# A hybrid delta-rule and HGRN2 block: values token-major in the front, pairs within a chunk on strips, keys transposed once for a pair of heads

## The chip, the cores and the metric

The kernel runs on one core of a Trainium2 chip. Five engines work side by side, each with its own queue of instructions: TensorE (PE in the profile, with its weight loads as PEld), VectorE (DVE), ScalarE (ACT), GpSimd (POOL) and SyncE (SP, which only issues DMAs here). They wait for one another through semaphores. The metric is the device time of one execution in microseconds (us).

## The reference

One layer of a hybrid backbone for 512 latent tokens and 256 context tokens, 1024 wide, in fp32:

```python
h_lat = rms_norm(x, norm_mix_g) * (1 + sc1) + sh1          # and h_ctx
(qkv, a_f, a_b, be_f, be_b, g_a, q_b, i_b, f_f, f_b, g_b, m_a, m_b) = split_last(h @ w_in, IN_SIZES)
...
# gated delta rule, chunked, 4 heads of 128, two directions
u_c = u_c - w_c @ s
s_next = gam_end_c * s + k_end_c.T @ u_c
o = qg_c @ s + att_c @ u_c
# HGRN2, chunked, 4 heads of 128, two directions; v = i_b, k = 1 - f
s_next = f_end_c * s + k_end_c.T @ v_c
pair = exp(where(incl, lg_c[i] - lg_c[j], -inf))
att = einsum('ik,jk,ijk->ij', q_c, k_c, pair)
o = (q_c * exp(lg_c)) @ s + att @ v_c
...
y = sigmoid(m_a) * (norm(oa) * silu(g_a)) @ w_up_a + sigmoid(m_b) * (norm(ob) * silu(g_b)) @ w_up_b
x = x + g1 * (y @ w_out)
x = x + g2 * swiglu(rms_norm(x, norm_ffn_g) * (1 + sc2) + sh2)
out = rms_norm(x, final_norm_g)
```

Each direction scans the context first and the latent tokens from the state that this leaves.

## The kernel before

**Projections.** Activations lie feature-major (features on partitions) as a high and a low part, `hhi, hlo` for the 512 latent tokens and `chi, clo` for the context. Every weight block is loaded by SP into one of two `raw` buffers (`split`, L84), rounded by ACT to `hi` (L100), and DVE makes the rest `lo` (L102). `mm3` (L105) then runs three matmuls for each 128 rows of the weight: hi x hi, hi x lo, lo x hi.

**The front**, up to the first key projection. `hhi` and `hlo` are made in eight steps, and in each step six gate projections (numbers 16 to 21) take their share into six banks `pg0`; their weights come as eight tiles `wr`. The 24 gates (two sets of 4 head gates, two of 8 merge gates) go to DRAM (`gdram`) and are read again by the up-projections. Behind it, at a priority put back by 1500 (so that they fill holes), two more gates are made, and sums for the modulation.

**The loops.** Streams are written as generators: `G0` and `G2` (`gdn_pair`, two heads of the delta rule each), `H0` to `H3` (`hgrn`, one head each), `F` (`filler`: one gate by `gate_low`, its matmuls at a priority put back by 1000), `N` and `aT` (modulation weights). The string `PLAN` says how many steps of each are written next; a scheduler then places each engine's instructions by that order, by priorities and by the buffers that come free. At `X` the delta rule's buffers are closed, all gates and modulation sums that are left are queued at low priority, and the rest of H2 runs, alone. Behind it come the up-projections (`pup`), `w_out` and the SwiGLU part (`pf`, `pfo`).

**One HGRN head** (`hgrn`, L484): two forget gates and the query are projected, log gates `L` and keys `K` are made on ACT and DVE. Then a ladder of levels: level 7 is the diagonal, and level l (block b = 1, 2, 4 ... 64) covers those pairs of a chunk of 128 tokens that lie in one block of 2b but not in one of b. For each level `kq` holds scaled keys and queries, `att` (L528) multiplies all 128 x 128 pairs of each of 4 chunks into the bank `pA`, and a predicated copy with the mask `lev` takes those of this level into `AT`; ACT copies the diagonal. After the ladder, `values` (L493) projects the head's values feature-major (24 matmuls of 512 and 24 of 256 columns), copies them, transposes six tiles into `pv` and copies those to `vh`. The scan over chunks then uses `AT` and `vh`.

**One delta-rule pair** (`gdn_pair`): after the inverses come six steps of two heads and two directions (L822 on). Each takes `pk` (a bank): the product of key and state, `rt`, the product with the inverse, then `u` (L837), a transpose of the key tile (L842), its copy scaled by decay (`kend`, L843) and their product (L844), which updates the state. Key tiles are transposed once for each direction. Outputs from `aT` and `u` (L853) go to `oa2`; `head_norm` (L469) squares, scales and transposes them into `pt` and stores y in `ydram`.

Of the kernel before, what the change touches and what calls it, by code (L numbers as in the profile page):

```python
# [13 lines left out]
P = 128  # L14
D = 1024
KT = 8
# [9 lines left out]
LEVELS = (1, 2, 4, 8, 16, 32, 64)  # L26
PADN = 8 * 68 + 260
# [4 lines left out]
        "F:1 G0:99 H0:99 F:3 G2:4 H1:99 G2:4 F:1 G2:99 N:1 H3:99 aT:1 H2:1 X H2:99")  # L32


def shape_constants():
    i = np.arange(P)
    r, c = i[:, None], i[None, :]
    sq = np.concatenate(
        [(r == c), (r <= c), (r >= c), (r < c), (r > c)], axis=1).astype(np.float32)
    lev = [(r // (2 * b) == c // (2 * b)) & (r // b != c // b) for b in LEVELS]  # L40
    return sq, np.concatenate(lev, axis=1).astype(np.uint8)
# [7 lines left out]
def body(tc, T, out, tap=None):  # L49
# [8 lines left out]
    with ExitStack() as root:  # L58
# [71 lines left out]
        ydram = dr.tile([8, P, SEQ], F32, name="ydram")  # L130
        gcols = [C_GA + P * i for i in range(4)] + [C_GB + P * i for i in range(4)]
# [45 lines left out]
        rest = [22, 23] + list(range(16))  # L177
# [3 lines left out]
        with ExitStack() as st:  # L181
# [174 lines left out]
            for d in range(KT):  # L356
# [20 lines left out]
            lev = cp.tile([P, 7 * P], U8, name="lev")  # L377
# [21 lines left out]
            for i in rest[0:2]:  # L399
                w = [s1.tile([P, KT, P], F32R, name=f"rw{i}{j}") for j in range(2)]  # L400
                w = split([W_IN[:, gcols[i]:gcols[i] + P]], KT, P, dst=[t[:, :, :] for t in w])
                gate_out(i, feat(w, lat, SEQ, f"pgate{i}"), sp, "gt")
            for q in quarters[0:4]:
# [80 lines left out]
        def hgrn(h):  # L484
# [8 lines left out]
            def values():  # L493
                w = split([W_IN[:, C_IB + P * h:C_IB + P * h + P]], KT, P)
                Z = hg.tile([P, TOK], F32, name=f"{n}Zv", tag="Z", bufs=2)
                for src, a, t in ((lat, CTX, SEQ), (ctx, 0, CTX)):
                    ps = feat(w, src, t, f"{n}zv_{a}")
                    nc.scalar.copy(Z[:, a:a + t], ps[:, 0:t])
                for g, cnt in ((0, 4), (4, 2)):
                    pv = pmm(f"{n}pv{g}")  # L500
                    for i in range(cnt):
                        nc.tensor.transpose(pv[:, P * i:P * i + P], Z[:, P * (g + i):P * (g + i + 1)], ident)
                    nc.scalar.copy(vh[:, g:g + cnt, :], pv[:, 0:P * cnt].rearrange("p (g k) -> p g k", k=P))

# [21 lines left out]
            AT = hg.tile([P, 4, P], F32, name=n + "AT", tag="AT")  # L526

            def att(kq, lvl):  # L528
                pA = bank("ha", f"{n}pA{lvl}")
                for c in range(4):  # L530
                    nc.tensor.matmul(pA[:, P * c:P * c + P], kq[:, 0, P * c:P * c + P], kq[:, 1, P * c:P * c + P],  # L531
                                     start=True, stop=True)
                if lvl == 7:
                    nc.scalar.copy(AT[:, :, :], pA.rearrange("p (c i) -> p c i", i=P))
                else:
                    nc.vector.copy_predicated(AT[:, :, :], lev[:, P * lvl:P * lvl + P].unsqueeze(1).to_broadcast([P, 4, P]),
                                              pA.rearrange("p (c i) -> p c i", i=P))
# [23 lines left out]
            values()  # L561
# [127 lines left out]
        def gdn_pair(h0):  # L689
# [127 lines left out]
            oa2 = gd.tile([P, 2, 4, P], F32, name=n + "oa", tag="blk", bufs=3)  # L817
            seen = set()
# [368 lines left out]
```

## Time and profile before

| what | before |
|---|---|
| median of 3 runs (lowest to highest) | 1082.74 us (1082.46 to 1085.16) |
| the profiled execution | 1084.9 us, span 1083.2 |
| granted clock, mean | 0.983 |
| first key projection (`g_k_zl`) begins | 102.4 us |
| last transposes of pair 2's norm | 508.5 us |
| first pairs of H2 (`h_pA`) | 545.9 us |
| last transposes of H2's norm | 580.25 us |
| up-projections at full speed | 615.5 us |

The page's windows give, for each stretch, the busy time of each engine and its instructions in brackets, the granted TensorE clock, the share of the DMA engines and what they moved. Rows of the timeline give the start, the length, the engine, the line, the tiles out<-in and the shape; a PE row's length includes the pipeline, so the distance of two starts is the price of one in a row of them. An fp32 product shows two records, a transpose one. The slices of the page (each 27 us, busy share in tenths) show how PE stands over the span:

```profile
PE   4999999889999999899989899999999999999996
```

### The profile page before, as it was taken

What the parts mean: (1) busy time and instruction counts of PE and PEld (TensorE: products, weight loads), DVE (VectorE), ACT (ScalarE), POOL (GpSimd) and SP (SyncE); (2) the same over time, 40 slices, a digit from 0 to 9 for tenths busy, and PEclk for the clock granted to TensorE, in tenths of its full rate; (3) what the DMA queues carried; (4) which work ended last, traced back from release to release, by engine and by line L of the source; (5) the groups of instructions that cost most, each with busy time, mean ns of one, the idle gap of its engine ahead of it and who ended that gap; (6) DMA issues with size and microseconds to landing.
All of it is one profiled execution on the core that took longest, in us unless ns stands there. A gap on an engine that the chain in (4) does not pass through costs nothing.

```text
span 1083.2 us, 16716 instructions
## 1 busy us (share of the span) xinstructions
PE 1018.9 (94%) x6567; PEld 843.8 (78%) x6567; DVE 659.3 (61%) x1246; ACT 549.2 (51%) x1037; POOL 72.4 (7%) x129
## 2 busy tenths in 40 slices
PE   4999999889999999899989899999999999999996
PEld 2587888777897887798767688798888878888785
DVE  3375686789767968875795565777343433422524
ACT  4373678658867765876764643442222222221212
POOL 1000000400001021001101000011000000000000
PEclk9999999989999999999899999999999999999998
DMA  9953222112004123102636643546333323322222
GB/s 315 344 182 114 60 57 61 50 58 69 3 25 142 50 68 88 51 2 96 203 120 220 226 157 119 154 138 192 96 98 94 97 84 98 97 97 97 89 97 87
DMA packets 139649, 121.72 MB, mean 112 GB/s; under 512 B 5533, under 2 KB 116531, under 8 KB 139571
## 3 DMA queue, kind: packets, MB, share of 16 engines
q1 hardware_dynamic: 133923, 104.05, 31.0%
q0 software_dynamic: 3552, 13.11, 3.6%
q10 hardware_dynamic: 2096, 3.50, 1.0%
q8 instruction: 51, 0.84, 0.3%
q14 instruction: 27, 0.22, 0.1%
HBM read 110.16 MB, written 10.49 MB: 111 GB/s over the span
## 4 chain that ended last, share of the span: by engine, by line
PE 43%; DVE 4%; DMA 4%; issue 3%; ACT 3%; POOL 1%; SPq 0%; POOLq 0%; ACTq 0%; DVEq 0%
PE pf L110 22%; PE pfo L110 10%; PE pup L110 3%; DMA uy<-ydram 1%; PE pgate L110 1%; PE pwo L110 1%; PE h_pA L531 1%; DMA mwb<-in_mod_w_dram 1%; DVE lo L102 1%; ACT hi L100 1%; PE p_s_pk L835 1%; PE p_s_pk L844 1%; DVE acc L878 0%; DMA ug<-gdram 0%; PE h_z L110 0%
## 5 line engine op out<-in xcount | busy, mean ns | idle before, releaser
L100 ACT CAST hi<-raw 128x1024 fp32r<-128x1024 f32 (+1 forms) x129 | 127.6, 991 | 274.2 <-PE pf L110 96.6
L102 DVE TENSOR_TENSOR lo<-raw,hi 128x1024 fp32r<-128x1024 f32 (+1 forms) x129 | 148.0, 1147 | 171.0 <-ACT hi L100 170.6
L110 PE MATMUL pf<-hhi,hi 128*128 128x512 f32 (+1 forms) x352 | 133.8, 381 | 0.0
L110 PE MATMUL pf<-hhi,lo 128*128 128x512 f32 (+1 forms) x352 | 133.7, 380 | 0.0
L110 PE MATMUL pf<-hlo,hi 128*128 128x512 f32 (+1 forms) x352 | 133.7, 380 | 0.0
L110 PEld LDWEIGHTS pf<-hlo,hi 128*128 128x128 f32 x352 | 66.2, 188 | 12.7 <-DVE hlo L1067 0.2
L110 PEld LDWEIGHTS pf<-hhi,lo 128*128 128x128 f32 x352 | 66.2, 188 | 12.7 <-DVE lo L102 0.2
L110 PEld LDWEIGHTS pf<-hhi,hi 128*128 128x128 f32 x352 | 66.1, 188 | 12.3
L110 PE MATMUL pfo<-lo,uh 128*128 128x512 f32 x176 | 68.8, 391 | 0.1
L110 PE MATMUL pfo<-hi,ul 128*128 128x512 f32 x176 | 68.5, 389 | 0.0
L110 PE MATMUL pfo<-hi,uh 128*128 128x512 f32 x176 | 67.9, 390 | 0.0
L110 PE MATMUL pgate<-hhi,hi 128*128 128x512 f32 x128 | 52.9, 413 | 4.1 <-ACT hi L100 4.0
L110 PE MATMUL pgate<-hhi,lo 128*128 128x512 f32 x128 | 52.4, 410 | 4.3 <-DVE lo L102 4.3
L110 PE MATMUL pgate<-hlo,hi 128*128 128x512 f32 x128 | 51.9, 405 | 0.0
L1123 DVE TENSOR_TENSOR sg<-sg,pf 128x512 f32<-128x512 f32 x22 | 15.1, 687 | 49.4 <-PE pf L110 49.4
L878 DVE SCALAR_TENSOR_TENSOR acc<-mwb,sc,acc 128x256 f32<-128x256 f32 x72 | 34.4, 480 | 9.9 <-DMA mwb<-in_mod_w_dram 8.6
L110 PE MATMUL h_z<-hhi,hi 128*128 128x512 f32 x96 | 39.7, 413 | 0.0
L110 PEld LDWEIGHTS pfo<-lo,uh 128*128 128x128 f32 x176 | 33.0, 188 | 7.8 <-DVE lo L102 1.0
L110 PE MATMUL h_z<-hlo,hi 128*128 128x512 f32 x96 | 39.0, 406 | 0.0
L110 PE MATMUL h_z<-hhi,lo 128*128 128x512 f32 x96 | 38.5, 401 | 0.0
L110 PEld LDWEIGHTS pfo<-hi,uh 128*128 128x128 f32 x176 | 32.8, 188 | 7.3 <-ACT hi L100 0.7
L110 PEld LDWEIGHTS pfo<-hi,ul 128*128 128x128 f32 x176 | 33.0, 188 | 6.8
(449 smaller groups left out, 2518.4 us busy)
## 6 DMA issues: line engine op xcount, KB each, us to landing
raw<-in_ffn_w_in_dram SPq DMA_DIRECT2D x44, 512.0 KB, 3.8
raw<-in_w_in_dram SPq DMA_DIRECT2D x37, 512.0 KB, 3.7
raw<-in_ffn_w_out_dram SPq DMA_DIRECT2D x22, 512.0 KB, 3.5
mwb<-in_mod_w_dram POOLq DMA_DIRECT2D x18, 512.0 KB, 4.7
mw<-in_mod_w_dram SPq DMA_DIRECT2D x16, 512.0 KB, 6.0
gdram<-gt SPq DMA_DIRECT2D x24, 256.0 KB, 2.2
raw<-in_w_in_dram SPq DMA_DIRECT2D x18, 256.0 KB, 2.9
mwe<-in_mod_w_dram SPq DMA_DIRECT2D x4, 1024.0 KB, 7.7
```

The lines of the kernel that those rows point to most:

```text
L100: nc.scalar.copy(hi[:, :, :], raw[:, :, :])
L102: nc.vector.tensor_tensor(lo[:, :, :], raw[:, :, :], hi.bitcast(F32), op=ALU.subtract)
L110: nc.tensor.matmul(ps, a[u](k), b[v](k), start=(start and n == 0), stop=(stop and n == tot - 1))
L531: nc.tensor.matmul(pA[:, P * c:P * c + P], kq[:, 0, P * c:P * c + P], kq[:, 1, P * c:P * c + P], start=True, stop=True)
L835: nc.tensor.matmul(pk[:, P:2 * P], N[:, d, e, g, :], rt[:, :], start=True, stop=True)
L844: nc.tensor.matmul(pk[:, 2 * P:3 * P], kend[:, :], u[:, :], start=True, stop=True)
L878: nc.vector.scalar_tensor_tensor(acc[:, :], mw[:, k - k0, :], sc[:, k:k + 1], acc[:, :], op0=ALU.mult, op1=ALU.add)
L1123: nc.vector.tensor_tensor(sg[:, :], sg[:, :], pgu[1][:, :], op=ALU.mult)
```

## The change

Three things, and the plan's numbers.

1. *Values.* In the front four of the six `pg0` banks now hold values of all heads: the activations stand still (128 tokens) and 512 columns of the weights for values stream, so the bank is token-major at once. The four gates that stood there (18 to 21) go to the head of `rest`; two of them are made at low priority where gates 22 and 23 were made, and the fillers get four more gates than before (20 for 16). Behind those two gates, at the same priority, the values of the context are made from four weight blocks, 48 matmuls of 128x512 into two banks `pv`. ACT copies the six tiles, SP stores them in `vdram`, and each head loads its own with one DMA into `vh`. The projection, copies and transposes of `values` go.
2. *Pairs.* For levels 0 to 4 and the diagonal `att` now multiplies only the blocks of 32 x 32 on the diagonal of each chunk: 16 products, each with 128 rows of contraction and 32 columns, in four column strips of PE. Level 5 takes the blocks beside them in the same shape, level 6 two blocks of 64 x 64 a chunk (8 products). The predicated copies work on `AD` (128 x 4 x 32); at level 4 four DVE copies put `AD` into `AT`, and levels 5 and 6 are copied by ACT.
3. *Keys of the delta rule.* The six key tiles of each head of a pair are transposed once, ahead of the steps, and copied by ACT (`kt`); the decay goes onto u instead: `ue` is u scaled by a product `nbe` of both factors, and plain `u` is made only where outputs need it.

`PLAN` gets three more fillers before X (12 for 9), and eight gates for seven are left behind it.

```diff
-        "F:1 G0:99 H0:99 F:3 G2:4 H1:99 G2:4 F:1 G2:99 N:1 H3:99 aT:1 H2:1 X H2:99")
+        "F:2 G0:99 H0:99 F:3 G2:4 H1:99 F:1 G2:4 F:2 G2:99 N:1 H3:99 aT:1 H2:1 X H2:99")
...
-        rest = [22, 23] + list(range(16))
+        rest = [18, 19, 20, 21, 22, 23] + list(range(16))
...
-                    nc.sync.dma_start(wr[:, :], W_IN[P * e:P * e + P, C_MB:C_MB + NG0 * P])
+                    nc.sync.dma_start(wr[:, 0:4 * P], W_IN[P * e:P * e + P, C_IB:C_IB + 4 * P])
+                    nc.sync.dma_start(wr[:, 4 * P:], W_IN[P * e:P * e + P, C_MB:C_MB + 2 * P])
...
-                    for i in range(NG0):
-                        nc.tensor.matmul(pg0[i][:, :], u[:, P * i:P * i + P], v[:, d, :],
-                                         start=(d == 0 and n == 0), stop=(d == KT - 1 and n == 2))
-            for i in range(NG0):
-                gate_out(16 + i, pg0[i], sp, "gt")
+                    for i in range(4):
+                        nc.tensor.matmul(pg0[i][:, :], v[:, d, P * i:P * i + P], u[:, 0:4 * P], **ends)
+                    for i in range(4, NG0):
+                        nc.tensor.matmul(pg0[i][:, :], u[:, P * i:P * i + P], v[:, d, :], **ends)
+            def value_out(g, ps):
+                vt = sp.tile([P, NH * P], F32, name=f"vt{g}", tag="gt", bufs=3)
+                nc.scalar.copy(vt[:, :], ps[:, :])
+                nc.sync.dma_start(vdram[g, :, :], vt[:, :])
...
+            pv = [pmm(f"pv{g}") for g in range(2)]
+            for kk in range(4):
+                w = split([W_IN[2 * P * kk:2 * P * kk + 2 * P, C_IB:C_IB + 4 * P]], 2, 4 * P)
+                for g in range(2):
+                    mm3(pv[g][:, :], [lambda k, t=t: t[:, 2 * kk + k, P * g:P * g + P] for t in ctx],
+                        [lambda k, t=t: t[:, k, :] for t in w], 2, start=(kk == 0), stop=(kk == 3))
+            for g in range(2):
+                value_out(g, pv[g])
...
             def att(kq, lvl):
+                w = 64 if lvl == 6 else NB
                 pA = bank("ha", f"{n}pA{lvl}")
                 for c in range(4):
-                    nc.tensor.matmul(pA[:, P * c:P * c + P], kq[:, 0, P * c:P * c + P], kq[:, 1, P * c:P * c + P],
-                                     start=True, stop=True)
+                    for j in range(P // w):
+                        kt0, qt0 = P * c + w * j, P * c + w * (j ^ (lvl in (5, 6)))
+                        nc.tensor.matmul(pA[w * j:w * j + w, w * c:w * c + w], kq[:, 0, kt0:kt0 + w], kq[:, 1, qt0:qt0 + w],
+                                         start=True, stop=True, tile_position=(0, w * j))
...
+                elif lvl < NSM:
+                    nc.vector.copy_predicated(AD[:, :, :], lev[:, NB * lvl:NB * lvl + NB].unsqueeze(1).to_broadcast([P, 4, NB]), pAv)
                 else:
+                    for j in range(P // w):
+                        s = slice(w * j, w * j + w)
+                        nc.scalar.copy(AT[s, :, w * (j ^ 1):w * (j ^ 1) + w], pAv[s, :, :])
+                if lvl == NSM - 1:
+                    for j in range(P // NB):
+                        s = slice(NB * j, NB * j + NB)
+                        nc.vector.tensor_copy(AT[s, :, s], AD[s, :, :])
...
-            values()
+            nc.sync.dma_start(vh[:, :, :], vdram[:, :, P * h:P * h + P].rearrange("g p v -> p g v"))
...
+                for g0, cnt in ((0, 2), (2, 4)):
+                    pt = bank("ga", f"{n}kt{e}{g0}")
+                    for i in range(cnt):
+                        nc.tensor.transpose(pt[:, P * i:P * i + P], KTt[:, g0 + i, :], ident)
+                    nc.scalar.copy(kt[:, g0:g0 + cnt, :], pt[:, 0:P * cnt].rearrange("p (g k) -> p g k", k=P))
...
-                        nc.scalar.activation(u[:, :], pk[:, P:2 * P], AF.Copy, scale=nbkv[:, g, d:d + 1])
+                        if step < 5:
+                            kt, nbe = kts[e]
+                            ue = gd.tile([P, P], F32, name=m + "ue", tag="ke", bufs=3)
+                            nc.scalar.activation(ue[:, :], pk[:, P:2 * P], AF.Copy, scale=nbe[:, g, d:d + 1])
                         if g >= 2:
+                            nc.scalar.activation(u[:, :], pk[:, P:2 * P], AF.Copy, scale=nbkv[:, g, d:d + 1])
...
-                            nc.tensor.transpose(pk[:, 2 * P:3 * P], KTt[:, g, :], ident)
-                            nc.scalar.activation(kend[:, :], pk[:, 2 * P:3 * P], AF.Copy, scale=dec[:, d, 1, g, h:h + 1])
-                            nc.tensor.matmul(pk[:, 2 * P:3 * P], kend[:, :], u[:, :], start=True, stop=True)
+                            nc.tensor.matmul(pk[:, 2 * P:3 * P], kt[:, g, :], ue[:, :], start=True, stop=True)
```

How the change moves instructions is shown at three places; names end in a running number, and lines of the kernel after are higher by some rows. PE, end of the front: before, the last deferred gate (`pgate_741`) goes directly over to `pab`, the projection of decay and beta, which stands ahead of the first key projection.

```order
L110 MATMUL pgate_741<-hhi,rw_735 128x512
L110 MATMUL pgate_741<-hlo,rw_735 128x512
L110 MATMUL pgate_741<-hhi,rw_736 128x512
L418 MATMUL pab_859<-chi,wab_855 32x256
L418 MATMUL pab_859<-clo,wab_855 32x256
```

After, at the same place (`hi_782` and `lo_784` are the first of the four weight blocks):

```order
L113 MATMUL pgate_750<-hhi,rw_745 128x512
L113 MATMUL pv_778<-hi_782,chi 128x512
L113 MATMUL pv_778<-lo_784,chi 128x512
L113 MATMUL pv_778<-hi_782,clo 128x512
L113 MATMUL pv_778<-hi_782,chi 128x512
L113 MATMUL pv_778<-lo_784,chi 128x512
```

46 of the 48 context-value matmuls stand between the gate and `pab`.

PE, the ladder of H2 with gates between its levels; before:

```order
L110 MATMUL pgate_5527<-hhi,lo_5525 128x512
L531 MATMUL h_pA_5943<-h_kqd 128x128 x4
L531 MATMUL h_pA_5954<-h_kq_5949 128x128 x4
L110 MATMUL pgate_5527<-hhi,hi_5523 128x512
L110 MATMUL pgate_5527<-hlo,hi_5523 128x512
L531 MATMUL h_pA_5967<-h_kq_5962 128x128 x4
```

After, the same place:

```order
L113 MATMUL pgate_5819<-hhi,hi_5815 128x512
L550 MATMUL h_pA_6270<-h_kqd 32x32 x16
L550 MATMUL h_pA_6293<-h_kq_6288 32x32 x16
L113 MATMUL pgate_5819<-hlo,hi_5815 128x512
L113 MATMUL pgate_5819<-hhi,lo_5817 128x512
L113 MATMUL pgate_5819<-hhi,hi_5815 128x512
L550 MATMUL h_pA_6318<-h_kq_6313 32x32 x16
```

Each call of `att` has 16 products of 32x32 in place of 4 of 128x128, and the gates between them stay.

ACT, from pair 2's last y (`p_oa<-p_1_pt`) on; before, the copies and exponentials of two projections of H2 stand there, with `h_kqd` still far behind:

```order
L481 ACTIVATE p_oa<-p_1_pt,vc 128x512
L516 ACTIVATE h_sg_5447<-h_sg_5447 128x768
L512 COPY h_Z_5835<-h_z_0_5837 128x512
L541 ACTIVATE h_Ed<-h_K,lno 128x512
L512 COPY h_Z_5835<-h_z_512_5863 128x256
L100 CAST hi_6042<-raw_6040 128x1024
L520 ACTIVATE h_sg_5447<-h_sg_5447 128x768
L522 ACTIVATE h_L<-h_sg_5447,lbo 128x768
```

After, the second forget gate is already copied (`h_Z_6161`), and the first keys (`h_kqd`) come four rows behind y:

```order
L506 ACTIVATE p_oa<-p_1_pt,vc 128x512
L527 ACTIVATE h_sg_6162<-h_Z_6161 128x768
L528 ACTIVATE h_sg_6162<-h_sg_6162 128x768
L529 ACTIVATE h_sg_6162<-h_sg_6162 128x768
L569 ACTIVATE h_kqd<-h_K,lno 128x512
L582 ACTIVATE h_kq_6288<-h_K,lno 128x2x256
L533 ACTIVATE h_sg_6162<-h_sg_6162 128x768
L525 COPY h_Z_6228<-h_z_0_6230 128x512
```

Counted to the last row that the first pairs need (the copy of `h_q` into `h_kqd`, further down), it was 29 rows from y before and is 17 now.

More of the change, by code (lines that the diff above doesn't have):

```diff
@@ L26 @@
 LEVELS = (1, 2, 4, 8, 16, 32, 64)
+NB = 32
+NSM = 5
 PADN = 8 * 68 + 260
@@ L364, in body @@
                 for n, (u, v) in enumerate(((wh, hhi), (wl, hhi), (wh, hlo))):
-                    for i in range(NG0):
-                        nc.tensor.matmul(pg0[i][:, :], u[:, P * i:P * i + P], v[:, d, :],
-                                         start=(d == 0 and n == 0), stop=(d == KT - 1 and n == 2))
-            for i in range(NG0):
-                gate_out(16 + i, pg0[i], sp, "gt")
+                    ends = dict(start=(d == 0 and n == 0), stop=(d == KT - 1 and n == 2))
+                    for i in range(4):
[6 more added lines that the diff above has]
+                nc.sync.dma_start(vdram[g, :, :], vt[:, :])
+            for i in range(4):
+                value_out(2 + i, pg0[i])
+            for i in range(4, NG0):
+                gate_out(12 + i, pg0[i], sp, "gt")
             for d in range(KT):
@@ L491, in hgrn @@
             vh = hg.tile([P, 6, P], F32, name=n + "v", tag="v")
[L493 to L503, printed above, removed]
             for d in range(3):
@@ L925, in run @@
                     break
-        gates = rest[2:]
+        gates = rest
         def filler(n):
```

20 lines of the change are left out of this document (14 added, 6 removed).

## The prediction

> **What bounds the kernel now.** I read the page's head, then the windows (busy time by stage), then the chain of work that ended last.
>
> ```profile
> span 1083.2 us, 16716 instructions
> PE 1018.9 (94%) x6567; PEld 843.8 (78%) x6567; DVE 659.3 (61%) x1246; ACT 549.2 (51%) x1037; POOL 72.4 (7%) x129
> core 0: us, PE busy (x) PEld busy (x) DVE busy (x) ACT busy (x) POOL busy (x), PEclk, DMA share, GB/s
> 0.00:102.40 102.40, 84.95 (x616) 59.21 (x616) 52.13 (x152) 44.46 (x75) 4.84 (x21) 0.98 0.78 247
> 102.40:508.50 406.10, 387.00 (x3221) 332.27 (x3222) 311.90 (x643) 292.12 (x639) 44.96 (x79) 0.98 0.19 55
> 508.50:545.90 37.40, 32.97 (x192) 27.23 (x191) 28.01 (x56) 26.36 (x47) 6.47 (x6) 0.91 0.69 215
> 545.90:565.50 19.60, 16.09 (x96) 13.55 (x97) 19.27 (x35) 13.41 (x19) 1.50 (x2) 0.97 0.36 127
> 581.20:615.50 34.30, 29.59 (x130) 23.84 (x128) 16.57 (x26) 20.98 (x31) 0.00 (x0) 1.00 0.69 233
> 545.23 0.63 ACT h_kqd L544
> 545.90 2.05 PE h_pA L531 x16
> 887.68 65.33 PE pf L110 x288
> ```
>
> The loops from 102.40 (first key projection) to 508.50 (pair 2's last norm) are bound by TensorE: 387.0 us busy of 406.1, so 19.1 idle; DVE and ACT reach 77% and 72%. There an instruction taken from PE is worth its spacing. The tail from 508.50 to 615.50 isn't: head H2 stands alone, its first pairs wait for ACT's keys (545.23), and from 545.90 DVE is busy 19.27 of 19.60. PE's gates fill the holes there. From the up-projections on, nothing is edited. The last row prices a 128x512 matmul: 65.33/288 = 0.227 us.
>
> The sum is made against the profiled execution, 1084.9 us (span 1083.2 and 1.7 around it), which is 0.2% above the median of 1082.74; the difference is carried to the median.
>
> **The change, before 508.50.**
>
> ```profile
> 347.29 0.28 PE L110 MATMUL g_v_zc<-clo,hi 128*128 128x256 f32 x1
> 347.41 0.28 PE L110 MATMUL g_v_zc<-chi,lo 128*128 128x256 f32 x1
> 347.53 1.05 PE L531 MATMUL h_pA<-h_kqd 128*128 128x128 f32 x8
> 348.42 1.06 PE L531 MATMUL h_pA<-h_kq 128*128 128x128 f32 x8
> ```
>
> Starts give 0.12 for a 128x256 matmul, and 0.89 for a call of att: eight records (two passes of four fp32 products) at 0.111. A transpose is one record, and I price it at 0.111 too.
>
> *Values.* In the front four of the six gate banks become values: the same 128x512 shape and count, so nothing changes there. Two of the deferred gates are still made there. New are the context's values: 4 blocks x 2 banks x 2 k x 3 = 48 matmuls, 48 x 0.227 = **+10.9**, and the order puts nearly all ahead of the first key projection, with nothing beside them that they could replace. Removed from each head: 24 x 0.227 + 24 x 0.12 + 6 transposes x 0.111 = 8.99; H0, H1 and H3 lie before 508.50: **−27.0**. Three more fillers (12 for 9) are put there: 3 x 24 x 0.227 = **+16.3**; its ends are 0, if all of them fall into the 19.1 us of PE's idle time, and 16.3. I take the whole, since PE's holes are the short waits between products and a filler behind them is already there. The four gates handed to the fillers balance the four value projections that leave the front, so the net of this part is only the two transposed shapes: 256-wide matmuls and transposes go.
>
> *Keys of the delta rule.*
>
> ```profile
> L842 PE MATMUL p_s_pk<-sq,g_KT 128*128 128x128 f32 x40 | 11.0, 279 | 0.0
> L843 ACT ACTIVATE p_s_ke<-p_s_pk,dec 128x128 f32<-128x128 f32 x40 | 14.6, 372 | 7.4 <-PE p_s_pk L842 7.1
> ```
>
> Forty transposes become 24: 16 x 0.111 = **−1.8**. ACT loses the 40 key copies and 16 of u and gets 40 of ue and 8 for the transposed keys. In 32 places u now stands behind ue on ACT, so its product with aT starts 0.372 later. ACT is 72% busy and the state's own chain takes ue first, so I cost this at nothing; the other streams' matmuls hide it. Without that cover it is 32 x 0.372 = 11.9, over four independent chains 3.0.
>
> *Strips.* A call of level 0 to 5 or 7 becomes 16 products of 32 columns, 32 records. No row shows K=128 with 32 columns streamed, so I bound it.
>
> ```profile
> 125.06 0.40 PE L110 MATMUL pgate<-hhi,lo 128*128 128x512 f32 x1
> 125.57 0.58 PE L116 MATMUL g_k_pn<-ones,g_k_acc 128*32 128x1 f32 x48
> 126.08 0.50 PE L110 MATMUL pgate<-hhi,hi 128*128 128x512 f32 x1
> 265.26 0.62 PE L778 MATMUL p_pR<-p_T,p_N 32*32 32x32 f32 x48 [1.28 <-DVE p_T L746]
> 265.81 0.50 PE L110 MATMUL g_k_zl<-hhi,hi 128*128 128x512 f32 x1
> 274.40:276.00 1.60, 1.60 (x31) 1.42 (x26) 1.28 (x4) 1.54 (x5) 0.00 (x0) 0.50 0.04 10
> 274.48 1.55 PE L803 MATMUL p_pRb<-p_X,p_N 64*64 64x64 f32 x24
> 275.96 1.22 PE L531 MATMUL h_pA<-h_kq 128*128 128x128 f32 x4
> 278.58 0.87 PE L803 MATMUL p_pRb<-p_X,p_N 64*64 64x64 f32 x24
> 279.37 0.71 PE L531 MATMUL h_pA<-h_kq 128*128 128x128 f32 x4
> ```
>
> The 32x32 tiles of p_pR take (265.81 − 265.26)/48 = 11.5 ns a record; the 128x32 strips of g_k_pn 10.6 ns, with one column moving. The 64x64 tiles take 33 ns, and 62 ns at a granted clock of 0.50. Going over to strips costs up to 125.57 − 125.06 − 0.227 = 0.28 us. So a call takes 32 x 0.0115 = 0.37 bare and 0.65 with the full passage. I take 0.55, the p_pR group's whole length, which is 0.18 for the passage: 21 calls x (0.55 − 0.89) = −7.1; ends −10.9 and −5.0. Level 6, eight products of 64x64, is 16 x 0.033 + 0.18 = 0.71: 3 x −0.18 = −0.5, ends −1.1 and −0.2. Together **−7.6** (−12.0 to −5.2).
>
> The Trainium skill (TensorE: Matmul & The Clock Gate, section "Wait — 56ns, not 53.3ns?") has a floor of about 25 ns from start to start however small a matmul is. By it a call would be 32 x 25 = 800 ns bare, 0.98 us with the passage, and the term would be about +2 in place of −7.1, so 1072 in all. The rows of tiles here (48 records in 0.55 us) go under that floor by more than half, so it gets no chance of its own. The same skill's TensorEngine Tiling (Array Packing), section "Key Properties", says that a change of tiling mode drains TensorE; the 0.28 us of the row at 125.57 agrees.
>
> Sum to 508.50: 10.9 − 27.0 + 16.3 − 1.8 − 7.6 = **−9.2**.
>
> **The change, in the tail.**
>
> ```profile
> 513.76 2.68 POOL p_hs L475
> 519.97 4.64 DMA mwb<-in_mod_w_dram
> 519.30:545.20 25.90, 25.47 (x159) 21.72 (x158) 21.86 (x41) 19.83 (x29) 3.81 (x5) 0.92 0.71 213
> L536 DVE COPY_PREDICATED h_AT<-lev,h_pA 128x512 f32<-128x512 uint8 x28 | 20.6, 737 | 3.3 <-PE h_pA L531 2.7 <-ACT h_AT L534 0.2
> L714 DVE SCALAR_TENSOR_TENSOR p_N<-p_pD,g_vec,p_E 128x128 f32<-128x128 f32 x48 | 14.6, 343 | 1.9 <-ACT p_E L712 1.6
> L795 DVE COPY p_X<-p_pX 32x192 f32<-32x192 f32 x8 | 2.8, 353 | 0.2
> 580.25 0.33 PE h__pt L480
> 607.26 6.78 DMA uy<-ydram
> 615.51 1.65 PE pup L110 x3
> PE pup L110 <- DVE x L1001: 4.7, 2, 3.8
> ```
>
> *ACT's rows.* Between pair 2's last y and H2's first keys ACT had 29 instructions, 19.83 us in the 25.90 of that stretch. In the new order H2's second forget gate is projected before pair 2's last transposes, and 17 rows are left: 12 x 0.684 = **−8.2**. Ends: −4.0, if DVE (21.86 busy) sets this stretch, and 12/29 x 25.90 = −10.7, if ACT's waits shrink with its rows. The chain of waits also runs through POOL (2.68) and a load of mod weights (4.64) here, which no row of ACT shortens, so I stay under the upper end.
>
> *The ladder.* Seven predicated copies of 128x512 at 0.737 become five of 128x128, which I price by L714's 0.343, and four DVE copies AT<-AD, each at most 0.353 (L795): 5 x 0.343 + 4 x 0.353 − 7 x 0.737 = **−2.0**, worth its full size only where DVE sets the pace, as at 545.90 to 565.50. Its end above is 0, if ACT, which takes over levels 5 and 6, sets it instead.
>
> *After H2.* 92 gate matmuls stood between its last transposes (580.25) and the up-projections; now 111. With the 36 pup recorded before the last wait that is 147 x 0.227 = 33.4, inside the 35.25 from 580.25 to 615.5, which the loads of uy set: 19 x 0.227 = 4.3 of work take the place of pup's wait of 4.7. **0**; ends −0.9, if the loads get faster and PE sets it (33.4 and 0.9 us of other work), and +4.3, if gate stores on SP ahead of uy push the last load back.
>
> Sum of the tail: **−10.2**. All: −9.2 − 10.2 = −19.4, so 1065.5 for the profiled run and **1063.3 us** as median. With every term at its end: gains −11.7 − 4.4 − 10.7 − 2.0 − 0.9, or 1082.74 − 26.9 = 1056; losses leave −9.2 + 2.4 − 4.0 + 0 + 4.3 = −6.5, or 1076. The zero of the fillers' term stands as a rival below.
>
> DMA brings 2 MB of weights forward into the front and 1.5 MB each way through vdram. Its share was 0.78 in the front and 0.19 later, so I cost this at nothing; if a front block comes late its whole price is below, under SP's order.
>
> **The rivals.**
>
> ```profile
> L102 DVE TENSOR_TENSOR lo<-raw,hi 128x1024 fp32r<-128x1024 f32 x111 | 135.6, 1222 | 164.6 <-ACT hi L100 164.2
> L100 ACT CAST hi<-raw 128x1024 fp32r<-128x1024 f32 x111 | 116.7, 1052 | 268.5 <-PE pf L110 96.6 <-PE pfo L110 71.3 <-issue 64.3
> raw<-in_w_in_dram SPq DMA_DIRECT2D x37, 512.0 KB, 3.7
> ```
>
> *Slower: strips at half clock.* The place is each ladder, where PE waits for the next pair. If strips come out behind a hole and the clock is 0.50 there, they cost 62 ns a record, as the row at 274.48: 32 x 0.062 + 0.18 = 2.16 a call, 1.61 over my value, times 28 calls, plus 4 x 16 x (0.062 − 0.033) = 1.9 for level 6: about **1110**. At 33 ns they would cost 0.69 x 28 more: **1083**. From 37 ns the kernel is slower than before by over 0.3%. For it: it was seen in this kernel; against it: the clock is 0.98 over the loops, and 11.5 ns were seen for four strips side by side. 0.08, half for each price.
>
> *The delta-rule's chain, not PE, sets the loops.* Then shorter PE work is idle time, the added 10.9 of the front stays, and only the tail gains: 1082.74 + 10.9 − 10.2 = **1083**. For it: 77% DVE and 72% ACT on dependent work. Against it: 95% PE. 0.10.
>
> *More gain: fillers fall into idle time.* The 16.3 shrinks by some 13 of PE's 19.1 idle: **1050**. For it: more fillers stand ready where PE waited; against it: nine were ready before and left those holes. 0.12.
>
> *SP's order.* The load of h_v waits for the one buffer, until the last product of the head before has read it, and SP holds the weight loads behind it. Each of three heads then shows one block bare, 3.7 + 1.05 + 1.22 = 6.0 us: 1063.3 + 18 = **1081**. 0.06. That the change doesn't do what it says (tiles not side by side) is the first rival's 33 ns.
>
> **How the numbers follow.** Forecast 0.64, with its own range of 1056 to 1076. To hold 8 in 10 the range must take in half of the 1050 case and most of the cases near 1083: 1052 to 1083. A measurement of this kernel can tell about 0.3% from no change, 1079.5 to 1086. Faster: 0.64 + 0.12 = 0.76. The cases at 1081 to 1083 hold 0.10 + 0.06 + 0.04 = 0.20, of which I put 0.06 above 1086, since two of them can come together: same 0.14, slower 0.04 + 0.06 = 0.10.
>
> **What would show it.** First key projection near 113 instead of 102.4; pair 2's last norm near 499; from there to the full up-projections some 97 instead of 107; a call of att near 0.55, no clock of 0.50 beside it; no SP wait of 6 us ahead of a weight load. If PE's busy share from the first key projection on falls well below 95% with the end near 1083, the second rival is right.

## The result and the profile after

The changed kernel took 1098.01 us (median of 4 runs, 1096.17 to 1100.06), the kernel before beside it 1083.95; the ratio is 1.0124 with an interval of 1.0107 to 1.0142. Forecast were 1063.3, so the change costs some 13 us (13.0 in the profiled runs) where 19 were to be gained. First the page of the kernel after: span, busy times, and its slices of PE's busy share and of the granted clock.

```profile
span 1096.2 us, 18073 instructions
PE 1010.1 (92%) x7183; PEld 821.3 (75%) x7183; DVE 655.2 (60%) x1265; ACT 555.0 (51%) x1050; POOL 71.2 (6%) x129
PE   4999999969897899979679999999999999999996
PEclk9999999999998999999889999999999999999998
```

TensorE is busy for 8.8 us less (1010.1 for 1018.9), and the span is 13.0 us longer (1096.2 for 1083.2): its idle time has grown. The same stages as before, in the windows of the kernel after:

```profile
core 0: us, PE busy (x) PEld busy (x) DVE busy (x) ACT busy (x) POOL busy (x), PEclk, DMA share, GB/s
0.00:113.20 113.20, 94.51 (x663) 67.57 (x663) 58.90 (x156) 50.84 (x83) 4.75 (x21) 0.98 0.76 242
113.20:524.90 411.70, 376.44 (x3682) 311.75 (x3671) 305.94 (x658) 296.39 (x647) 45.35 (x79) 0.98 0.22 64
524.90:555.00 30.10, 19.26 (x105) 14.29 (x104) 21.90 (x46) 19.23 (x38) 3.51 (x4) 0.74 0.66 210
555.00:571.90 16.90, 14.19 (x280) 10.21 (x279) 15.54 (x34) 12.27 (x22) 0.75 (x1) 0.96 0.26 86
571.90:589.60 17.70, 15.94 (x82) 13.36 (x82) 11.42 (x26) 7.60 (x24) 4.01 (x5) 0.81 0.56 176
589.60:616.40 26.80, 26.80 (x116) 21.51 (x117) 17.67 (x29) 16.84 (x26) 1.53 (x2) 1.00 0.84 275
```

| stage (profiled runs) | before | after | difference | forecast |
|---|---|---|---|---|
| to the first key projection | 102.4 | 113.2 | +10.8 | +10.9 |
| from there to pair 2's norm | 406.1 | 411.7 | +5.6 | −20.1 |
| to H2's first pairs | 37.4 | 30.1 | −7.3 | −8.2 |
| H2's ladder | 19.6 | 16.9 | −2.7 | −2.0 |
| to H2's last transposes | 14.8 | 17.7 | +2.9 | 0 |
| to the first up-projection | 21.9 | 26.8 | +4.9 | 0, with the next row |
| up-projections, to `w_out` | 54.0 | 52.8 | −1.2 | |
| the rest | 427.0 | 427.0 | 0 | 0 |

The front and H2's first two stages came as forecast. Of 32.4 us missing, 25.7 lie in the loops and 6.6 behind H2's ladder. One mark is not what its name says, here, in the table of times before and in the prediction: at 508.5 (524.9 after) come the transposes of the first of pair 2's two heads, and the last ones come at 516.9 (530.9 after). Counted to these, the loops lose 3.2 us for 5.6, and the stage behind them gains 4.9 for 7.3. In the loops PE had 387.0 of 406.1 us busy before and 376.4 of 411.7 now: 10.6 us of busy time are gone, and 16.2 of idle time have come.

### The profile page after: what moved, and what is told of

Same layout as the page of the kernel before. It is cut to its first block, busy times and chain, and to the rows that moved or that the text cites. A ratio compares the mean times of both kernels' runs of the same rounds, so it can differ in the third digit from the quotient of the medians.

```text
span 1096.2 us, 18073 instructions
## 1 busy us (share of the span) xinstructions
PE 1010.1 (92%) x7183; PEld 821.3 (75%) x7183; DVE 655.2 (60%) x1265; ACT 555.0 (51%) x1050; POOL 71.2 (6%) x129
## 4 chain that ended last, share of the span: by engine, by line
PE 67%; DVE 11%; issue 7%; DMA 6%; ACT 6%; POOL 2%; SPq 1%; POOLq 0%; ACTq 0%; DVEq 0%
PE pf L113 22%; PE pfo L113 10%; PE h_z L113 5%; PE pgate L113 5%; PE pup L113 3%; PE pg L372 2%; DVE lo L105 2%; DMA mwb<-in_mod_w_dram 2%; PE g_q_zl L113 2%; DMA mwe<-in_mod_w_dram 1%; PE p_pD L734 1%; PE g_k_zl L113 1%; PE pg L374 1%; PE p_s_pk L874 1%; ACT hi L103 1%
## 5 line engine op out<-in xcount | busy, mean ns | idle before, releaser
L103 ACT CAST hi<-raw 128x1024 fp32r<-128x1024 f32 (+1 forms) x136 | 132.3, 975 | 283.5 <-PE pf L113 99.3
L105 DVE TENSOR_TENSOR lo<-raw,hi 128x1024 fp32r<-128x1024 f32 (+1 forms) x136 | 154.3, 1135 | 172.3 <-ACT hi L103 171.5
L113 PE MATMUL pgate<-hhi,hi 128*128 128x512 f32 x160 | 69.5, 435 | 12.1 <-ACT hi L103 12.0
L113 PE MATMUL pgate<-hhi,lo 128*128 128x512 f32 x160 | 68.4, 429 | 8.4 <-DVE lo L105 7.9
L113 PEld LDWEIGHTS pf<-hhi,lo 128*128 128x128 f32 x352 | 66.2, 188 | 12.5
L113 PE MATMUL pgate<-hlo,hi 128*128 128x512 f32 x160 | 67.5, 422 | 0.0
L113 PEld LDWEIGHTS pgate<-hhi,hi 128*128 128x128 f32 x160 | 32.2, 201 | 21.3 <-ACT hi L103 15.6
L113 PEld LDWEIGHTS pgate<-hhi,lo 128*128 128x128 f32 x160 | 32.1, 200 | 19.0 <-DVE lo L105 13.0
```

Of the source, the lines that this page charges most:

```text
L103: nc.scalar.copy(hi[:, :, :], raw[:, :, :])
L105: nc.vector.tensor_tensor(lo[:, :, :], raw[:, :, :], hi.bitcast(F32), op=ALU.subtract)
L113: nc.tensor.matmul(ps, a[u](k), b[v](k), start=(start and n == 0), stop=(stop and n == tot - 1))
```

## The experiments

All ratios are to the kernel before on the same chip. Fifteen kernels ran. Each trace is one execution, and executions of one kernel differ by up to 0.8% (1081.2 to 1089.4 us for the kernel before, in the runs beside e13), so a few us between two traces show little.

**A stall that was seen.** The chain of waits in the kernel after, around the first pair's norm:

```profile
332.17 7.92 DMA mwe<-in_mod_w_dram
340.12 0.61 DVE mwe L166 x2
340.74 1.65 DVE mwe L168 x5
...
343.26 2.35 POOL p_hs L500
345.64 0.41 ACT p_on L502
346.09 0.48 PE p_pt L505
```

A modulation load that takes 7.92 us holds VectorE, whose next row but a few is the second head's norm; that holds GpSimd, ScalarE's scaling and PE's transposes. In the windows, PE has no instruction in 342 to 346, and then a granted clock of 0.50:

```profile
342.00:346.00 4.00, 0.00 (x0) 0.00 (x0) 2.72 (x7) 0.36 (x2) 2.34 (x1) 0.82 0.00 0
346.00:350.00 4.00, 3.91 (x72) 2.96 (x73) 0.33 (x2) 2.50 (x7) 0.48 (x1) 0.50 0.02 4
```

The Trainium skill (TensorE: Matmul & The Clock Gate, Part 1, "What's actually happening") says that the clock is halved after an idle window of about 3.4 us; the trace agrees here, with 5.40 us idle ahead of the transposes at 346.09 and a clock of 0.50 behind them.

The rows of SP in the same stretch: the first row holds the stores of both heads' y, of which the second waits for that norm, and the next weight load comes behind it, at 354.37.

```profile
338.04 11.97 SPq L507 DMA_DIRECT2D ydram<-p_oa  x2
354.37 0.38 SPq L95 DMA_DIRECT2D raw<-in_w_in_dram  x1
```

The stretch from this norm (336.0) to the second pair's first decay products (386.6) takes 50.6 us for 40.4 before. The first experiment takes the stall out of the kernel after:

```diff
+            powed.append(ss)          # head_norm, behind the power on GpSimd
...
+            mw = gd.tile([P, 12 if tag == "N" else KT, 256], F32, name=f"mwe{sec}{j}", tag=tag)
+            if tag == "N":
+                nc.gpsimd.tensor_copy(mw[:, 0, 0:4], powed[-1])
-        ... "F:2 N:1 G0:1 H0:2 " "F:2 G0:99 H0:99 ..."
+        ... "F:2 G0:1 H0:2 " "F:2 G0:99 N:1 H0:99 ..."
```

> The kernel after, with one edit: the two modulation loads into the tile N start only when GpSimd has made the power of the second head's norm, so that their products stand behind that norm on VectorE. Theory A (collision: between the first pair's norm and the second pair's first decay products, 336.0 to 386.6 us in the trace after, VectorE stands 3.2 us at a late modulation load ahead of the norm, PE idles 5.4, its clock goes to 0.50 and SP's stores of y hold the weight loads; 10 to 16 of the 25 us lost lie there): 10 to 16 us faster than the kernel after, about 1082 to 1088, with that stretch near 38 instead of 50.6. Theory B (the dependent chains of the loops set the pace, so that cuts on PE come out as idle time anywhere): within 3 us of the kernel after, 1095 to 1098, the lost time only moves. Theory C (SP holds weight loads behind the waits of the h_v loads): no change either, the waits of 40 and 31 us on SP stay.

Measured: 1.015 (1.0119 to 1.018), no faster than after. The stretch went to 44.4 us (339.3 to 383.7), but the next one, from the second pair's first decay products to its inverse, grew from 81.8 to 88.1 (383.7 to 471.8). Theory A falls: the stall was real, and was not what the time hung on.

**The parts, each alone on the kernel before.**

```diff
 e2: values in the front, vdram, h_v loads, four gates to the fillers; old att, old keys, old PLAN
 e3: att on strips, AD, small lev; nothing else
 e4: kt, nbe and ue in gdn_pair; nothing else
```

> The kernel before with only the values moved into the front (old pairs, old key transposes, old plan, so that 11 gates are left behind X instead of 7). PE-paced loops: front +10.9, loops -27.0, four more gates behind H2 +21.8 less what fills H2's holes (some 10 to 15 of idle time): 1077 to 1085. Theory B: front +10.9 and little back in the loops, 1090 to 1097. Theory C: the h_v loads are in this kernel, so it shows the same long waits of SP at the h_v load and is above 1090; the other parts alone don't.

> The kernel before with only the pairs on strips. The trace after shows 0.39 us from a call of 32 records to the next instruction (forecast 0.55, before 0.89). PE-paced loops: 21 x (0.39 - 0.89) = -10.5 and about -3 on H2's ladder, 1068 to 1074. Theory B: only the ladder of H2 gains, 1080 to 1084. Theory A says nothing of it unless the scan's end moves against the modulation load.

> The kernel before with only the key tiles of the delta rule transposed once. PE-paced loops: -1.8, so 1081. Theory A: the scan's last steps get shorter, the modulation load (issued when the tile N is read for the last time) lands later against the norm, and the kernel gets slower by 3 to 16 us although nothing else is added: 1086 to 1098. Theory B: the chain per step loses a transpose and a copy, so 2 to 6 us faster, 1077 to 1081.

Measured: values 1.0297 (1.0281 to 1.0312), strips 0.9934 (0.9916 to 0.9953), keys 0.9986 (0.9969 to 1.0004). Times 1085 us, that is +32.2, −7.2 and −1.5. The values alone cost more than the whole change. In e2 the stretch of pair 2 from its decay products to its inverse took 93.1 us (382.0 to 475.1) for 80.8 before.

Theory C had an answer without a run of its own: SP does wait long at the h_v loads, but hardly a weight was late for it. In the waits of ScalarE, which casts each block first, the raw loads account for 1.3 us in all between 200 and 620 us of the kernel after. No run moved these loads to another queue or gave them a second buffer.

**The values left out, and H3 held.** e5 is the kernel before without any projection of values: 27 us of TensorE's work go from the loops and 9 from the tail, with the casts, remainders and copies that ScalarE and VectorE made for it, and nothing comes in but a load of h_v for each head. e6 adds a hold, by which H3's ladder can't start before pair 2's inverse. e7 is the hold on the kernel after, and e8 the kernel after with the old plan.

```diff
-            values()
+            nc.sync.dma_start(vh[:, :, :], W_IN[0:6 * P, C_IB + P * h:C_IB + P * h + P].rearrange("(g p) v -> p g v", p=P))
...
+            held[h0] = T2             # gdn_pair, behind the last transpose of the 32-blocks
...
+            if h == 3:                # hgrn, ahead of the ladder
+                nc.vector.tensor_copy(E[:, 0:1], held[2][:, 0, 0:1])
```

> The kernel before with the projection, copies and transposes of the values left out altogether (each head loads its 384 KB from the weights instead, so the outputs of the HGRN heads are not the reference's); front, plan, pairs and keys as before. PE-paced loops: 27.0 us of TensorE's work go before 508.5 and 9 more in the tail with nothing put in: 1047 to 1058. Theory D (in the loops VectorE and its order set the end: the values were a brake on the HGRN heads; without them a head's ladder comes out ahead of the second pair's inverse in VectorE's order, as in the run with the values alone, where 8 level copies instead of 4 stand between that pair's first decay products and its inverse, and the stretch takes 93.1 instead of 80.7 us): little or nothing is gained, 1075 to 1095.

> As the run with the values left out, and H3's ladder can't start before the second pair's blocks of 32 are inverted (a one-column copy on VectorE from that pair's tile into the ladder's first tile E). Theory D: 6 to 12 us faster than without the hold, the stretch from the second pair's decay products to its inverse back at 75 to 82 us. If VectorE's order isn't the cause: within 3 us of the run without the hold, or slower since H3 ends later.

> The kernel after with the same hold on H3's ladder. Theory D: the stretch from the second pair's decay products (386.6) to its inverse (468.4) gets 5 to 10 us shorter, and the kernel 4 to 10 faster: 1088 to 1094. Otherwise within 3 us of 1098, or slower.

> The kernel after with the plan of before: 9 fillers before X instead of 12, so 11 gates behind it. If the parts simply add (values alone x1.0297, strips x0.9934, keys x0.9986) it is x1.021, 1106 to 1110, and the new plan is worth some 9 us, because the fillers fill holes and the gates at the end stand bare. If the three fillers cost their 16.3 us in the loops, as the forecast had it, it is 1085 to 1092 (16.3 less, but up to 12 more behind H2).

Measured: e5 1.0003 (0.9982 to 1.0025), e6 0.9922 (0.9897 to 0.9946), e7 1.0218 (1.0181 to 1.0255), e8 1.0169 (1.0144 to 1.0195).

e5 asks the question most directly. Its windows, for the loops, the tail to `w_out`, and 28 us around pair 2's inverse:

```profile
102.50:523.30 420.80, 385.12 (x3116) 327.41 (x3116) 310.14 (x644) 292.66 (x632) 44.52 (x79) 0.94 0.19 55
523.30:658.90 135.60, 114.63 (x638) 91.23 (x638) 99.42 (x179) 76.99 (x134) 9.82 (x12) 0.91 0.61 196
448.00:476.00 28.00, 16.21 (x305) 14.01 (x306) 19.57 (x42) 16.28 (x36) 0.91 (x2) 0.51 0.01 2
```

With 27 us of matmuls less the loops got longer, 420.8 for 406.1 us. TensorE's busy time fell by 2 us only (385.1 for 387.0). For one thing, more of H2's projections fall into the longer stretch (414 records of `h_z` for 357, 85.1 us for 73.5). For another, what is left ran slower: the mean clock is 0.94 for 0.98, which is some 50 us at half clock for some 16 (twice 0.06 of 420.8, twice 0.02 of 406.1). The tail gained what the loops lost: H2's first pairs come at 546.8 for 545.9.

The h_v loads aren't the reason. SP waits 82 us for them in e5, but ScalarE waited for a weight only ahead of 333.2 (3.0 us) and 541.0 (2.3). Between 430 and 476 us, where TensorE stands idle most, it waits 8.5 us for H3's keys from VectorE (`h_kq`) and 3.9 for pair 2's blocks from ScalarE (`p_T`), and for no weight to land.

Where pair 2 lost time shows in VectorE's level copies. The windows for the tile `h_AT` alone (columns PE, PEld, DVE, ACT), from pair 2's first decay products to its inverse; the kernel before, then e5, then e6:

```profile
367.60:448.40 80.80, 1.54 (x8) 1.21 (x8) 2.39 (x4) 0.59 (x1) 1.00 0.23 66
```

```profile
371.00:465.60 94.60, 1.54 (x8) 1.22 (x8) 5.84 (x8) 0.59 (x1) 0.87 0.18 53
```

```profile
367.60:442.80 75.20, 1.55 (x8) 1.22 (x8) 0.73 (x1) 0.00 (x0) 0.92 0.23 67
```

Without the values H3's ladder comes earlier, and eight level copies instead of four (with each of them the level's other rows) stand on VectorE ahead of pair 2's inverse. The hold takes that back, 75.2 us for 94.6, and the kernel gains 0.8% over e5. So the values' time on TensorE had also kept H3 behind pair 2. But this is no rule for the other kernels: in e7 the same stretch fell as expected, from 81.8 to 72.3 (393.9 to 466.3), while H3's last transposes went from 513 to 540 us and H2's first pairs from 555.0 to 573.3, and the kernel lost 1%. There are two chains, pair 2's and H3's with H2 behind it, and what VectorE does first for the one delays the other. (The executions that were profiled took 1081.67 us in e6, 0.6% over its median, and 1112.14 in e7, 0.3% over.)

e8 shows what the plan is worth in the changed kernel: the three fillers, which the forecast priced at +16.3 in the loops, save 0.45% of the whole, about 5 us (1.0169 against 1.0124). The traces say where: from the first key projection to H2's first pairs the kernel after takes 12.1 us more than e8 (441.8 for 429.7), and from there to the first up-projection 20.5 less (61.4 for 81.9), since three gates fewer stand there.

**What each term costs.** e9 is strips and keys together, e10 with the hold, e11 the kernel after without the context's values, e12 the kernel before with half of the delta rule's substitution left out:

```diff
 e11:
-            pv = [pmm(f"pv{g}") for g in range(2)]
-            ... value_out(g, pv[g])
+            nc.sync.dma_start(vh[:, 0:2, :], W_IN[0:2 * P, C_IB + P * h:C_IB + P * h + P].rearrange("(g p) v -> p g v", p=P))
             ...
 e12:
             for r in range(1, 31):
+                if r < 16:
                     ...
```

> The kernel before with pairs on strips and keys transposed once, and nothing of the values' move (front, values and plan as before). If the parts add (x0.9934 and x0.9986): x0.992, about 9 us below before. If the keys' shorter scan and the strips get in each other's way through VectorE's order: x0.996 to 1.002.

> Strips and keys on the kernel before, and H3's ladder held until the second pair's inverse begins. Theory D as the run with the values left out showed it (hold worth x0.992): 4 to 9 us below the run without the hold, x0.984 to 0.988. If holding H3 makes H2's start late, as in the kernel after with the hold (x1.0218 against 1.0124): x0.995 to 1.003.

> The kernel after with the context's values left out (four weight blocks, 48 matmuls, their copies and stores; each head's context tiles come from the weights, so the HGRN outputs aren't the reference's). The front's +10.8 shown by the trace is bare time: 9 to 13 us faster than after, ratio to before 1.000 to 1.004, with the first key projection back at 102 to 103. If the loops behind absorb it (waits at the same later events): 1.007 or more.

> The kernel before with half of the 30 serial steps of the delta rule's 32-blocks left out (30 of the 60 small VectorE operations of each pair, about 10 us a pair; the inverse isn't the reference's). Nothing goes from TensorE. If the loops are bound by TensorE, as the prediction had it: within 2 us of before (0.998 to 1.000). If VectorE and the pairs' chain on it set the end (theory D): 8 to 16 us faster, 0.985 to 0.993.

Measured: e9 0.9946 (0.9926 to 0.9965), e10 1.003 (1.0011 to 1.0049), e11 1.0002 (0.9985 to 1.002), e12 0.993 (0.9903 to 0.9957).

e11: the context's values cost 1.2%, 13 us, all of them bare; without them the first key projection is at 102.1 again, and the rest of the change comes to nothing. e10: the hold costs 0.8% on strips and keys, as it cost 1% in e7.

e12 takes nothing from TensorE. In the groups by line these two are the operations of the substitution, in the kernel before:

```profile
L739 DVE TENSOR_TENSOR p_Z<-p_Z,p_o 128x30 f32<-128x30 f32 (+14 forms) x60 | 19.7, 329 | 1.3
L737 DVE TENSOR_TENSOR p_o<-p_Z 128x30 f32<-128x30 f32 (+14 forms) x60 | 19.6, 326 | 2.5 <-POOL p_Z L732 1.4
```

and in e12:

```profile
L740 DVE TENSOR_TENSOR p_Z<-p_Z,p_o 128x30 f32<-128x30 f32 (+14 forms) x30 | 9.9, 331 | 0.7
L738 DVE TENSOR_TENSOR p_o<-p_Z 128x30 f32<-128x30 f32 (+14 forms) x30 | 9.9, 328 | 3.2 <-POOL p_Z L732 2.6
```

19.5 us of VectorE's chain less gave 7.6 us (1086.26 x 0.007). In e5 36 us of TensorE's work less gave nothing. Neither fits loops bound by TensorE alone. But e12 doesn't show that pair 2's chain sets the end. In its trace that pair's last transposes come 19.5 us earlier (497.4 for 516.9), H3's 19.4 later (516.4 for 497.0), and H2's first pairs only 0.7 earlier (545.2 for 545.9). Most of the 4.7 us that the profiled run gains lies in the up-projections (49.6 for 54.0), and why isn't known.

**Do the holes take fillers?** If the values stood in holes, other fillers in their place should be free, and leave the stretch behind H2. e13 is e9 with the new plan (12 fillers, 4 gates behind X), e14 with 14 fillers and 2 gates behind, e15 is e5 with the new plan.

> Strips and keys on the kernel before, with the plan of after: 12 gates before X instead of 9, 4 behind it. If TensorE's work in the loops is paid at its spacing, the three gates cost 16.3 there and bring at most as much behind H2: x0.995 to 1.003. If the loops have idle time on TensorE that fillers fill at no cost (theory E): the three gates' 16.3 leave the stretch behind H2, and 5 to 14 us are gained: x0.982 to 0.990.

> As the run with 12 fillers, with 14 before X and 2 behind it. Theory E: 2 to 8 us below the run with 12, x0.977 to 0.986, until H2's own waits stand bare for want of gates. If fillers are paid: equal or slower, also through VectorE's remainders of the weights (1.22 us for a gate).

> The values left out (as before) with the plan of after, 12 fillers before X: three gates' work stands where the values' work was, nothing else is new. Theory E (the values' 27 us stood in holes that wait for VectorE, ScalarE and the pairs' chain; taken out they leave idle time, and a clock of 0.50 in 54.5 us of the loops against 13.6 before): 10 to 18 us below the run without the three, x0.984 to 0.991. If instead TensorE's work is paid: x0.998 to 1.004.

Measured: e13 0.9994 (0.9969 to 1.0018), e14 1.0066 (1.0043 to 1.0089), e15 0.9896 (0.9859 to 0.9932). The windows of e15, loops and tail to `w_out`:

```profile
105.00:518.80 413.80, 388.50 (x3175) 329.48 (x3175) 312.89 (x649) 295.34 (x640) 45.57 (x79) 0.97 0.22 61
518.80:645.00 126.20, 101.48 (x577) 80.05 (x578) 95.88 (x176) 73.75 (x129) 10.43 (x13) 0.91 0.60 194
```

Against e5 the loops hold three gates more (72 matmuls, 16.3 us at their spacing) and take 7.0 us less, at a clock of 0.97 for 0.94; the tail is 9.4 shorter. Where the values' work is still in the loops (e13 and e14), three fillers more cost 5 us and five cost 13, as ratios to e9. That the holes hold about what the values filled fits these three runs.

It doesn't fit the kernel after, as a mark shows that lies on H2's own path, H2's first pairs:

| kernel (profiled run) | first key projection | H2's first pairs | between them | first up-projection |
|---|---|---|---|---|
| before | 102.4 | 545.9 | 443.5 | 602.2 |
| e2, values moved | 114.9 | 556.5 | 441.6 | 641.9 |
| e3, strips | 102.5 | 543.6 | 441.1 | 600.2 |
| e4, keys | 103.1 | 549.9 | 446.8 | 610.2 |
| e5, values left out | 102.5 | 546.8 | 444.3 | 604.7 |
| e12, half substitution | 103.3 | 545.2 | 441.9 | 601.1 |
| e9, strips and keys | 101.0 | 544.6 | 443.6 | 601.3 |
| e13, e9 with 12 fillers | 102.7 | 557.3 | 454.6 | 604.9 |
| e14, e9 with 14 fillers | 102.1 | 565.8 | 463.7 | 610.8 |
| e8, all three parts, 9 fillers | 115.7 | 545.4 | 429.7 | 627.3 |
| after (12 fillers) | 113.2 | 555.0 | 441.8 | 616.4 |
| e15, e5 with 12 fillers | 105.0 | 542.9 | 437.9 | 591.1 |

Between the two marks a part alone brings next to nothing: 443.5 us before, 441.1 to 446.8 in e2 to e5, and no more with half the substitution left out (e12). Together the parts bring 13.8 (e8). So the values were worth something once strips and keys were there (13.9, e8 against e9), and strips and keys once the values were gone (11.9, e8 against e2). The ratios agree: strips and keys take 0.5% off the kernel before (e9) and 1.2% off e2 (1.0169 against 1.0297). Work that is put in is paid for most of its spacing: three fillers, 16.3 us, cost 12.1 in the kernel after (against e8) and 11.0 in e13, five, 27.2 us, cost 20.1 in e14. Only on e5 were they free, and why there alone no run shows.

No run beats the strips alone (0.9934) or with the keys (0.9946) while computing the whole; these two can't be told apart and beat both the kernel before and the kernel after.

## Why the prediction was wrong, by its own steps

- **The bound.** "There an instruction taken from PE is worth its spacing" is the sentence that failed. Up to H2's first pairs the forecast took 36.4 us off TensorE (27.0 + 1.8 + 7.6) at full worth; without the new fillers 13.8 came (e8). The fillers then cost 12.1, so that of the 28.3 forecast up to that mark (20.1 and 8.2) 1.7 were left. The 26.6 missing there are most of the 32.4. A busy share of 95% was read as a bound. It says only that something was always at hand: the scheduler had put independent projections into the waits of the pairs' and heads' chains, and PE's busy time stretches when its clock falls. The row that could have warned is this one of the kernel before, just ahead of pair 2's inverse, in which VectorE (42.27 of 46.40 us) is as busy as PE (42.75):

```profile
402.00:448.40 46.40, 42.75 (x231) 35.71 (x231) 42.27 (x90) 29.83 (x49) 6.45 (x9) 1.00 0.29 85
```

  VectorE's share of 77% over the whole loops hid it.
- **Values, −27.0.** This is the term that was most mis-sized: nothing when they leave the kernel before (e5), and 13.9 in the loops when they leave the kernel with strips and keys (e8 against e9). That the four gates "balance the four value projections that leave the front" was wrong with it: the projections that left were worth little, and the gates that came cost most of their spacing. e2 adds up by this: e5's 0, a front later by 12.5 (first key projection at 114.9) and four bare gates behind X (4 x 24 x 0.227 = 21.8) are 34; measured were 32.2.
- **Fillers, +16.3.** Near in the loops: 12.1 in the kernel after. The end of 0 and the rival with 1050 had them fall into idle time; that came only on e5 (e15). That the plan still gains 5 us (e8) is because a gate that isn't a filler stands bare behind H2.
- **Context's values, +10.9.** Right: +10.8 in the trace, 13 by e11. This term is as large as the whole loss of the change.
- **Strips, −7.6 and −2.0.** Near as a sum: −7.2 (−9.1 to −5.1) for −9.6. But that was luck: in the trace of e3 only 2.4 us lie ahead of H2's first pairs (441.1 from the first key projection), and 4.8 in the up-projections (49.2 for 54.0), which strips don't touch. The call itself was cheaper than priced. From one call's start to the next instruction, the kernel after, and at the end the group of the predicated copies (297 ns, priced at 343):

```profile
374.77 0.46 PE L550 MATMUL h_pA<-h_kq 128*32 128x32 f32 x32
375.16 0.50 PE L113 MATMUL h_z<-hhi,lo 128*128 128x512 f32 x1
...
382.20 0.69 PE L550 MATMUL h_pA<-h_kq 128*64 128x64 f32 x16
382.82 0.39 PE L113 MATMUL h_z<-chi,hi 128*128 128x256 f32 x1
L556 DVE COPY_PREDICATED h_AD<-lev,h_pA 128x128 f32<-128x128 uint8 x20 | 5.9, 297 | 4.4 <-PE h_pA L550 4.1
```

  0.39 us for 32 records, the lower end almost, and 0.62 for a 64x64 call (0.71 forecast). By 0.50 a call, 24 calls before 508.5 should have given over 10; 2.4 came there in e3, which is again TensorE's time being worth less than its spacing.
- **Keys, −1.8.** −1.5, but the interval reaches zero.
- **Tail, −10.2.** To H2's first pairs −7.3 for −8.2, in the ladder −2.7 for −2.0: right in size. But the first is counted from pair 2's norm, which came late; from the first key projection H2's first pairs came 1.7 earlier in all, and no run shows that fewer rows of ACT are the cause. The second was lost again in the scan. The 111 gates were to be hidden by pup's wait. They weren't: the first up-projection came 4.9 later (19 x 0.227 = 4.3) and only 1.2 came back. H2's scan after the ladder took 2.9 more, at a clock of 0.81; why, no run tried.
- **The rivals.** The second, with the chain instead of PE as the bound (1083, chance 0.10), came nearest: less work on PE did become idle time (PE's share in the loops fell to 91%). Its time was too low, since it kept the tail's −10.2 and let the gates that moved cost nothing, and which chain sets the end isn't shown. Strips ran at half clock in three calls only (H2's first two, 0.45 and 0.56 us, and H3's last), and behind SP's waits one weight was late, by 1.3 us.
- **A slip in the sum.** The gains "−11.7 − 4.4 − 10.7 − 2.0 − 0.9" add up to −29.7; with the sum's own −9.2 in place of −11.7 it is −27.2, or 1055.5 for the 1056 that was given. Nothing hangs on it.

What stays open is what sets the pace of the loops in TensorE's place. The hold returns 9 of the 27 us that e5 should have gained, and the half clock goes along with the idle time (e15, with three fillers more, has 0.97). How much of the remaining 18 is the slower clock and how much the pairs' and heads' chains on VectorE and ScalarE wasn't separated, nor why the parts bring more together than alone.

## What to carry to other kernels

A busy share of 95% doesn't tell what an instruction less is worth: here independent projections, put into waits by a scheduler, filled the engine. Work taken out of such loops can be worth nothing while work put in costs most of its spacing, so price the two apart. Leaving the work out altogether is one run and shows what moving it alone can bring; but parts can be worth more together than alone (e8), so leave it out of the kernel with the other parts as well. A stage with nothing beside it (here the front) pays in full for whatever is moved there.

## What the runs showed of the hardware that was not expected

Column strips of 128x32 with 32 columns streamed cost 12 ns a record (0.39 us for 32), with hardly any price for going over to them, although the row of g_k_pn had shown up to 0.28. And the granted clock can stay at half for long without a long idle time: in e5 it averaged 0.51 from 448 to 476 us, with PE busy 16.2 of 28.0 us and no idle time in it longer than 3.9.
